# A weight block's first sum by an accumulating transfer, and seven products in four of eight row pairs of the MLPs

## The chip, the cores and the metric

The kernel runs on one core of one Trainium2 chip. The metric is device time in microseconds (us), as the median of repeated executions. The engines of the core are named as the profile names them: PE (TensorE, matrix multiplies; PEld its weight loads), DVE (VectorE), ACT (ScalarE), POOL (GpSimd) and SP (SyncE, which only issues transfers here). Transfers (DMA) are issued from a queue of SP or of POOL and share the core's 16 DMA engines.

## The reference

A decoder trunk of two layers over 256 positions of width 2048, all in float32. Layer 0 is retention with 8 heads, layer 1 latent attention with 16 heads; each is followed by an MLP with a squared ReLU of width 8192. Cut to what the change touches:

```python
def sq_relu_mlp(h, w1, w2):
    return jnp.square(jax.nn.relu(h @ w1)) @ w2

def reference(x, ...):
    for layer in range(2):
        if layer == 0:
            x = x + retention(rms_norm(x, norm_mix[0]), ret_w_in, ret_w_out, cos, sin)
        else:
            x = x + mla_attention(...)
        x = x + sq_relu_mlp(rms_norm(x, norm_mlp[layer]), mlp_w1[layer], mlp_w2[layer])
```

## The kernel before

**Float32 by two parts.** Each operand is split into a high part rounded for the PE (`wh`, a cast on ACT, line 185) and a low part (`wl`, the rest, a subtraction on DVE, line 186). A product of two 128-row blocks is then three matmuls: high by high, high by low, low by high (lines 356 to 358).

**Row pairs and column pairs.** The large weights stand in HBM as chunks of 1 MB, one for each row pair: 256 rows by 1024 columns, as four 128x512 blocks side by side in the order b11, b12, b22, b21 (128 partitions x 2048 elements). `gemm_pair` computes one column pair: it runs over its row pairs (eight in the MLPs), calls `quad` for each, and accumulates in PSUM. The 256 positions are two halves, so each row pair is a two-by-two block product. It takes eight products, or seven by a scheme of sums and differences of blocks: the activations' sums come from `with_sums` (line 392 on, kept in `more`), and the weights' sums are made in `quad`.

**One row pair in `quad`.** SP loads the chunk into `raw` (line 285; four buffers). For eight products there are two splits of 128x1024 and 24 matmuls. For seven there are four splits (128x1024, 128x512, 128x1024, 128x1024), three additions on DVE that make the weights' sums in place in `raw` (lines 321, 324, 325), and 21 matmuls. The parts have five buffers each (`wh`, `wl`), which bounds how far ACT and DVE run ahead of PE. `raw` is freed by its last split, and SP then loads the row pair that stands four further on.

**Which row pairs have seven.** `kinds` says it for each column pair. `THREE` is (3, 5, 7), `FOUR` is (1, 3, 5, 7), `HEAD` is (2, 4, 6, 7). Retention's gate and value projections (`rp`, one column pair a head) and the first half of its output projection (`ro`) use `HEAD`.

**The MLP.** `mlp` (line 784 on) walks four groups. A group has two column pairs of the up projection (`u`, p = 0 to 7 over the layer) and two of the down projection (`d`, p = 0 and 1), each over the group's eight row pairs. What ends an up pair (`pair_out`, `summed`, `up`, `turn`) runs in the first row pairs of the next column pair: ACT copies six accumulators out of PSUM (line 373), DVE joins them (lines 375 to 380 and 389), ACT applies the ReLU (797), PE transposes (205), ACT squares (806), and the blocks `hid` are split and, where a later seven needs it, summed (lines 396 to 398, `hid_sum`, `hid_more`).

**x's home.** The residual stream stands in HBM. A down pair that isn't of the last group adds its eight blocks there (`to_home`, line 150) by eight accumulating transfers of 256 KB from POOL's queue, also in the first row pairs of the next column pair; two go to each home block, and the second waits until the first has landed. The last group brings x back (`x_tiles`, line 140), adds, and writes it (line 474).

**Order.** Each engine works through its instructions in one fixed order, which a list scheduler chose when the program was built; an engine that waits holds up all that stands behind it. POOL's order holds the transfers that it issues and the small steps of the norms (lines 163 and 165).

Names: c11, c12, c21, c22 are the accumulators of the four result blocks, p1, p5, p6 and p7 those of the further products of the seven scheme, and u and v what `pair_out` joins from them.

Of the kernel before, what the change touches and what calls it, by code (L numbers as in the profile page):

```python
# [16 lines left out]
ALU = mybir.AluOpType  # L17
# [3 lines left out]
P = 128  # L21
# [25 lines left out]
NOPE, ROPE, MV, KVR, QR = 128, 64, 128, 512, 1536  # L47
KV_NBS, Q_NB = (320, 256), 384
GROUPS = (4, 4, 4, 4)
THREE, FOUR, HEAD = (3, 5, 7), (1, 3, 5, 7), (2, 4, 6, 7)  # L50
PI = math.pi

G_MIX0, G_MLP0, G_KV, G_MIX1, G_MLP1 = 0, 16, 32, 48, 64
# [15 lines left out]
def yoco(ctx: ExitStack, tc: tile.TileContext, a):  # L69
    nc = tc.nc  # L70
# [3 lines left out]
    def f2k(shape, name, dtype=F32):  # L74
        return pool.tile([P, *shape], dtype, tag="f2k", bufs=14, name=name)
# [15 lines left out]
    def act_tile(name, dtype=F32R):  # L91

        return pool.tile([P, 2, 2, S], dtype, tag="act", bufs=24, name=name)
# [5 lines left out]
    def later(n, fn):  # L99
        queue.append((clock[0] + n, next(count), fn))  # L100
# [11 lines left out]
    def need(items, n):  # L112
        while len(items) < n:
            run_first()
# [18 lines left out]
    def x_tiles(name):  # L133


        def bring(b):
            both = act_tile(f"x_{name}{b}", F32)
            for t in range(NT):
                x[t][b] = both[:, t].rearrange("p i s -> p (i s)")
                nc.gpsimd.dma_start(x[t][b], x_home[t][b])  # L140

        for b in range(NB):
            later(2 * b, lambda b=b: bring(b))
# [38 lines left out]
    def split(h, l, src, scale=None):  # L182

        if scale is None:
            nc.scalar.copy(h, src)  # L185
            nc.vector.tensor_tensor(l, src, h.bitcast(F32), op=ALU.subtract)  # L186
        else:
            nc.scalar.activation(h, src, AF.Copy, scale=scale)
            nc.vector.scalar_tensor_tensor(
                l, src, scale, h.bitcast(F32), op0=ALU.mult, op1=ALU.subtract  # L190
            )

    def split_act(v, src, scales=(None, None)):
        if scales == (None, None):
            split(v[:, :, 0], v[:, :, 1], src)
        else:
            for j in range(2):
                split(v[:, j, 0], v[:, j, 1], src[:, j], scales[j])

    def transposed(srcs, name):  # L200

        tp = bank("tp", [2, S], name)
        for j in range(2):
            for t in range(NT):
                nc.tensor.transpose(tp[:, j, t * P : (t + 1) * P], srcs(t, j), ident)
        return tp
# [75 lines left out]
    def quad(w, chunk, x, mm, name):  # L282

        raw = pool.tile([P, 2048], F32, tag="raw", bufs=4, name=f"{name}_raw")
        nc.sync.dma_start(raw, w[chunk])
        v, more = x

        def a(t, k):
            return [v[:, k, i, t * P : (t + 1) * P] for i in range(2)]

        def s(n):
            return [more[:, n // 2, i, n % 2 * P : (n % 2 + 1) * P] for i in range(2)]

        b = raw.rearrange("p (i n) -> p i n", i=4)

        def parts(src, part):
            n = src.free_size() // 512
            wh, wl = (
                pool.tile([P, 2, 512], F32R, tag=f"w{i}", bufs=5, name=f"{name}_w{i}{part}")[:, :n] for i in "hl"
            )  # L300
            split(wh, wl, src)
            return [[i[:, j] for i in (wh, wl)] for j in range(n)]

        b11, b22 = parts(b[:, 0:3:2], 0)
        if more is None:
            mm("c11", a(0, 0), b11)
            mm("c21", a(1, 0), b11)
            mm("c12", a(0, 1), b22)
            mm("c22", a(1, 1), b22)
            b12, b21 = parts(b[:, 1:4:2], 1)  # L310
            mm("c12", a(0, 0), b12)
            mm("c22", a(1, 0), b12)
            mm("c11", a(0, 1), b21)
            mm("c21", a(1, 1), b21)
            return
        mm("p1", a(0, 0), b11)
        mm("c12", s(3), b22)
        (b21,) = parts(b[:, 3:4], 1)
        mm("c11", a(0, 1), b21)

        nc.vector.tensor_tensor(  # L321
            b[:, 0:2], b[:, 0:3:2], b[:, 1].unsqueeze(1).to_broadcast([P, 2, 512]), op=ALU.add
        )
        nc.vector.tensor_tensor(b[:, 2], b[:, 0], b[:, 2], op=ALU.add)
        nc.vector.tensor_tensor(b[:, 3], b[:, 2], b[:, 3], op=ALU.add)
        u1, u3 = parts(b[:, 0:2], 2)
        mm("p5", s(1), u1)
        mm("p7", s(0), u3)
        u2, u4 = parts(b[:, 2:4], 3)
        mm("p6", s(2), u2)  # L330
        mm("c21", a(1, 1), u4)
# [53 lines left out]
    def summed(c):  # L385

        for row in c:
            for block in row:
                nc.vector.tensor_tensor(block[0], block[0], block[1], op=ALU.add)
        return [[block[0] for block in row] for row in c]  # L390

    def with_sums(blocks, name):

        blocks = blocks.rearrange("p j (t n) -> p (j t) n", t=NT)
        sums = f2k([4, P], f"{name}_sum")
        nc.vector.tensor_tensor(sums[:, 0:2], blocks[:, 0:2], blocks[:, 1:4:2], op=ALU.subtract)
        nc.vector.tensor_tensor(sums[:, 2], sums[:, 1], blocks[:, 0], op=ALU.subtract)
        nc.vector.tensor_tensor(sums[:, 3], blocks[:, 2], sums[:, 2], op=ALU.add)
        more = act_tile(f"{name}_more")
        split_act(more, sums.rearrange("p (j t) n -> p j (t n)", j=2))  # L400
        return more
# [4 lines left out]
    def gemm(w, chunk0, act, nk, nb, name, done, before=None):  # L406

        acc = accs(nb, name)
        n = nk // 4
        for g in range(n - 1):  # L410
            piece(w, chunk0 + g, acc, act, g, nk, nb, name, before)
        last_piece(w, chunk0, acc, act, nk, nb, name, done, before)
# [328 lines left out]
    for h in range(RH):  # L741
# [35 lines left out]
        kinds = HEAD if h > 1 else HEAD[1:]  # L777
# [6 lines left out]
    def mlp(layer, act, r, done):  # L784
        w1, w2 = a[f"mlp_w1_{layer}"], a[f"mlp_w2_{layer}"]
        f0 = 0
        for gi, nf in enumerate(GROUPS):
            hid, blocks = [], []
            last = gi == len(GROUPS) - 1

            def up(c, p, hid=hid, blocks=blocks, last=last):

                need(r, NT)
                c = summed(c)
                for t in range(NT):
                    for i in range(2):
                        nc.scalar.activation(c[t][i], c[t][i], AF.Relu, scale=r[t])

                def turn(i):
                    for q in (2 * i, 2 * i + 1):  # L800
                        name = f"hid{layer}_{p}{q}"
                        tp = transposed(
                            lambda t, j: c[t][q // 2][:, (q % 2 * 2 + j) * P : (q % 2 * 2 + j + 1) * P], f"{name}_tp"
                        )
                        u = f2k([2, S], f"{name}_u")
                        nc.scalar.activation(u, tp, AF.Square)
                        v = act_tile(name)
                        split_act(v, u)
                        blocks.append((v, with_sums(u, name) if len(blocks) in (THREE if last else FOUR) else None))
                        hid.append(v)  # L810

                later(0, lambda: turn(0))
                later(1, lambda: turn(1))

            for p in range(f0 // 2, (f0 + nf) // 2):
                kinds = THREE[not (p or layer) :] if p % 2 or not p else FOUR
                gemm_pair(
                    w1, p * 8, act, [i in kinds for i in range(8)], f"u{layer}_{p}", lambda c, p=p, up=up: up(c, p)
                )
            if last:  # L820
                x_tiles(f"mlp{layer}")
            for p in range(2):
                if last and p and layer:
                    for b in (2, 3):
                        need(hid, 2 * nf)
                        gemm(
                            a["mlp_w2t"], (b - 2) * nf, hid, 4 * nf, 512, f"d{layer}_{gi}{b}",
                            lambda acc, b=b: done(b, acc),
                        )
                    continue  # L830

                def add(c, p=p, last=last):
                    into_x(done, c, p) if last else to_home(c, p)

                kinds = [i in (FOUR if p and not last else THREE) for i in range(2 * nf)]
                gemm_pair(w2, p * 32 + 2 * f0, blocks, kinds, f"d{layer}_{gi}{p}", add)
            f0 += nf

# [347 lines left out]
```

## Time and profile before

| | us |
|---|---|
| median of 3 runs | 2477.24 (2477.16 to 2477.25) |
| profiled execution | 2474.51 |
| its span | 2472.7 |

The profile is of one execution. Its span runs from the first to the last instruction of the program. In its lists, "L321 DVE u_raw<-u_raw" is the work of line 321 of the kernel on DVE, with buffer numbers left out of the names; a row ends with a count, busy time and mean, or, in a timeline, with the idle time before it and what ended that. What the stages take in the span:

| stage | us from the span's start |
|---|---|
| inputs, first head's gate | 0 to 90 |
| retention, heads | 90 to 625 |
| its output projection, second half | 625 to 720 |
| MLP of layer 0 | 720 to 1396 |
| latent attention | 1396 to 1770 |
| MLP of layer 1 | 1770 to 2472 |

The lines of the page on transfers and its list of transfer issues:

```profile
DMA  9555567555564685684785564445545856857854
GB/s 328 211 174 205 196 205 234 199 192 201 198 236 182 209 262 216 213 254 172 246 263 196 192 228 168 153 155 179 199 174 199 261 212 209 268 203 225 266 192 153
...
u_raw<-in_mlp_w SPq DMA_DIRECT2D x128, 1024.0 KB, 5.2
d_raw<-in_mlp_w SPq DMA_DIRECT2D x120, 1024.0 KB, 4.9
rp_raw<-in_ret_w_gv SPq DMA_DIRECT2D x56, 1024.0 KB, 4.9
```

The first row has the mean busy share of the 16 DMA engines in tenths, in 40 slices of the span. In the last three rows stand the count, the size, and the median us from issue to landing.

### The profile page before, as it was taken

Reading aid. Unit: us, or ns where it says so; the run is one execution under the profiler, and the core shown is the slowest. Engines: PE = TensorE matmul, PEld = TensorE weight load, DVE = VectorE, ACT = ScalarE, POOL = GpSimd, SP = SyncE. Lnnn points to the kernel's source line nnn. Section 1 sums busy time; section 2 is a strip of 40 time slices with the busy share of each in tenths; the row PEclk is TensorE's granted clock in tenths of the full one; section 3 lists DMA queues with packets and bytes.
Section 4 is the critical chain, followed back from the end, with each engine's and each line's share of the span. In section 5 each row is a group of like instructions: output and inputs, shape, how many; then the busy total and the mean of one; then the engine's idle time right before and its main releaser. Section 6 shows DMA issues by size and latency. Waiting matters only on the chain.

```text
span 2472.7 us, 31711 instructions
## 1 busy us (share of the span) xinstructions
PE 2455.6 (99%) x11635; PEld 2060.0 (83%) x11635; DVE 2167.4 (88%) x2805; ACT 1606.1 (65%) x2253; POOL 251.6 (10%) x310
## 2 busy tenths in 40 slices
PE   9999999999999999999999999999999999999999
PEld 7888888888888888888888888998888888888887
DVE  7799899889899999999999967776689999999996
ACT  6566656556676667667666766676566666676663
POOL 7300011000010010110110101110000201101100
PEclk9999999999999999999999999999999999999999
DMA  9555567555564685684785564445545856857854
GB/s 328 211 174 205 196 205 234 199 192 201 198 236 182 209 262 216 213 254 172 246 263 196 192 228 168 153 155 179 199 174 199 261 212 209 268 203 225 266 192 153
DMA packets 93403, 521.04 MB, mean 211 GB/s; under 512 B 11072, under 2 KB 12224, under 8 KB 40000
## 3 DMA queue, kind: packets, MB, share of 16 engines
q1 hardware_dynamic: 71856, 472.83, 53.8%
q0 software_dynamic: 21248, 46.15, 8.5%
q8 instruction: 91, 1.49, 0.2%
q14 instruction: 64, 0.52, 0.1%
q10 hardware_dynamic: 144, 0.05, 0.0%
HBM read 479.14 MB, written 39.85 MB: 210 GB/s over the span
## 4 chain that ended last, share of the span: by engine, by line
PE 91%; DVE 4%; ACT 3%; issue 1%; POOL 1%; DMA 0%; SPq 0%; ACTq 0%; POOLq 0%; DVEq 0%
PE u_c L358 7%; PE u_c L356 7%; PE u_c L357 7%; PE d_c L357 6%; PE d_c L358 6%; PE d_c L356 6%; PE rk_acc L274 2%; PE rq_acc L274 2%; PE rp_c L356 2%; PE rp_c L357 2%; PE rp_c L358 2%; PE u_p L358 2%; PE u_p L356 2%; PE u_p L357 2%; PE d_p L356 2%; PE d_p L358 2%
## 5 line engine op out<-in xcount | busy, mean ns | idle before, releaser
L185 ACT CAST u_wh<-u_raw 128x1024 fp32r<-128x1024 f32 x362 | 347.9, 991 | 207.8 <-DVE u_raw L321 100.8
L185 ACT CAST d_wh<-d_raw 128x1024 fp32r<-128x1024 f32 x358 | 344.1, 993 | 202.5 <-DVE d_raw L321 93.9
L186 DVE TENSOR_TENSOR u_wl<-u_raw,u_wh 128x1024 fp32r<-128x1024 f32 x362 | 402.0, 1144 | 47.2 <-ACT u_wh L185 41.7
L186 DVE TENSOR_TENSOR d_wl<-d_raw,d_wh 128x1024 fp32r<-128x1024 f32 x358 | 397.8, 1146 | 40.1 <-ACT d_wh L185 35.5
L356 PE MATMUL u_c<-u_wh,n 128*128 128x512 f32 x706 | 276.4, 392 | 0.0
L357 PE MATMUL u_c<-u_wl,n 128*128 128x512 f32 x706 | 275.5, 390 | 0.0
L358 PE MATMUL u_c<-u_wh,n 128*128 128x512 f32 x706 | 274.9, 389 | 0.0
L356 PE MATMUL d_c<-d_wh,hid 128*128 128x512 f32 x654 | 256.0, 392 | 0.0
L357 PE MATMUL d_c<-d_wl,hid 128*128 128x512 f32 x654 | 255.4, 391 | 0.0
L358 PE MATMUL d_c<-d_wh,hid 128*128 128x512 f32 x654 | 254.6, 389 | 0.0
L185 ACT CAST rp_wh<-rp_raw 128x1024 fp32r<-128x1024 f32 (+1 forms) x166 | 160.7, 982 | 140.9 <-DVE rp_raw L321 64.9
L186 DVE TENSOR_TENSOR rp_wl<-rp_raw,rp_wh 128x1024 fp32r<-128x1024 f32 (+1 forms) x166 | 184.9, 1137 | 26.7 <-ACT rp_wh L185 24.4
L358 PEld LDWEIGHTS u_c<-u_wh,n 128*128 128x128 f32 x706 | 132.6, 188 | 27.4
L356 PEld LDWEIGHTS u_c<-u_wh,n 128*128 128x128 f32 x706 | 132.6, 188 | 26.9
L357 PEld LDWEIGHTS u_c<-u_wl,n 128*128 128x128 f32 x706 | 132.6, 188 | 26.7
L358 PEld LDWEIGHTS d_c<-d_wh,hid 128*128 128x128 f32 x654 | 122.8, 188 | 25.4
L356 PEld LDWEIGHTS d_c<-d_wh,hid 128*128 128x128 f32 x654 | 122.8, 188 | 25.2
L357 PEld LDWEIGHTS d_c<-d_wl,hid 128*128 128x128 f32 x654 | 122.9, 188 | 24.7
L150 POOL DMA_DIRECT2D xh<-d_c x48 | 41.6, 867 | 856.6 <-ACT d_c L373 854.7
L185 ACT CAST ro_wh<-ro_raw 128x1024 fp32r<-128x1024 f32 x88 | 85.7, 997 | 59.7 <-DVE ro_raw L321 25.7
L356 PE MATMUL rp_c<-rp_wh,a 128*128 128x512 f32 x286 | 111.9, 391 | 0.0
L357 PE MATMUL rp_c<-rp_wl,a 128*128 128x512 f32 x286 | 111.4, 390 | 0.2 <-DVE rp_wl L186 0.2
(465 smaller groups left out, 6075.6 us busy)
## 6 DMA issues: line engine op xcount, KB each, us to landing
u_raw<-in_mlp_w SPq DMA_DIRECT2D x128, 1024.0 KB, 5.2
d_raw<-in_mlp_w SPq DMA_DIRECT2D x120, 1024.0 KB, 4.9
rp_raw<-in_ret_w_gv SPq DMA_DIRECT2D x56, 1024.0 KB, 4.9
ro_raw<-in_ret_w_out SPq DMA_DIRECT2D x32, 1024.0 KB, 4.9
uq_raw<-in_mla_w_uq SPq DMA_DIRECT2D x24, 768.0 KB, 4.1
rq_raw<-in_ret_w_qk SPq DMA_DIRECT2D x16, 1024.0 KB, 5.0
rk_raw<-in_ret_w_qk SPq DMA_DIRECT2D x16, 1024.0 KB, 4.8
wo_raw<-in_mla_w_o SPq DMA_DIRECT2D x16, 1024.0 KB, 4.8
```

Source lines behind the costliest of these rows:

```text
L150: nc.gpsimd.dma_start(x_home[t][2 * p + j], part, accum_op=ALU.add)
L185: nc.scalar.copy(h, src)
L186: nc.vector.tensor_tensor(l, src, h.bitcast(F32), op=ALU.subtract)
L274: nc.tensor.matmul(acc[f], wh[:, cols], a.rearrange("p i s -> p (i s)"), start=k == 0, stop=k == nk - 1)
L356: nc.tensor.matmul(dst, ah, bh, start=n == 0, stop=False)
L357: nc.tensor.matmul(dst, ah, bl, start=False, stop=False)
L358: nc.tensor.matmul(dst, al, bh, start=False, stop=n == total[key] - 1)
```

## The change

1. In `quad`, where a row pair has seven products, POOL issues an accumulating transfer inside SBUF that adds b11 to b12 in place (256 KB), in every stage that uses sevens. The first DVE addition, which made b11 + b12 and b12 + b22 at 128x1024, goes. DVE now adds b22 to that sum (128x512), takes b11 off again for b12 + b22 (128x512), and adds b21 as before (128x512). The two sums change places in `raw`, so `u1` and `u3` are named the other way round.
2. `FOUR` becomes (2, 3, 5, 7). It also says which activation blocks have sums, so block 2 has them in place of block 1.
3. In the MLPs, all up pairs but p = 0 use `FOUR` (before, the odd ones and p = 0 used `THREE`; in layer 0, p = 0 has (5, 7) before and after), and all down pairs but the last group's use `FOUR` (before, only p = 1). That is 14 more row pairs with seven: 157 in place of 143 in the whole kernel.

```diff
-THREE, FOUR, HEAD = (3, 5, 7), (1, 3, 5, 7), (2, 4, 6, 7)
+THREE, FOUR, HEAD = (3, 5, 7), (2, 3, 5, 7), (2, 4, 6, 7)
...
         nc.sync.dma_start(raw, w[chunk])
         v, more = x
+        if more is not None:
+            nc.gpsimd.dma_start(raw[:, 512:1024], raw[:, 0:512], accum_op=ALU.add)
...
-        nc.vector.tensor_tensor(
-            b[:, 0:2], b[:, 0:3:2], b[:, 1].unsqueeze(1).to_broadcast([P, 2, 512]), op=ALU.add
-        )
-        nc.vector.tensor_tensor(b[:, 2], b[:, 0], b[:, 2], op=ALU.add)
+        nc.vector.tensor_tensor(b[:, 2], b[:, 1], b[:, 2], op=ALU.add)
+        nc.vector.tensor_tensor(b[:, 0], b[:, 2], b[:, 0], op=ALU.subtract)
         nc.vector.tensor_tensor(b[:, 3], b[:, 2], b[:, 3], op=ALU.add)
-        u1, u3 = parts(b[:, 0:2], 2)
+        u3, u1 = parts(b[:, 0:2], 2)
...
-                kinds = THREE[not (p or layer) :] if p % 2 or not p else FOUR
+                kinds = FOUR if p else THREE[1 - layer :]
...
-                kinds = [i in (FOUR if p and not last else THREE) for i in range(2 * nf)]
+                kinds = [i in (THREE if last else FOUR) for i in range(2 * nf)]
```

In the changed kernel the transfer is line 288 and the three additions are lines 323, 324 and 325. In the built program's order on POOL, in a column pair that follows a down pair, the transfer for row pair 2 stands behind the first home transfer, the one for row pair 3 behind the third, and those for row pairs 5 and 7 behind all eight.

## The prediction

> **What bounds the kernel now.** I read the page first, then stage windows, then TensorE's timeline matmul by matmul.
>
> ```profile
> span 2472.7 us, 31711 instructions
> ...
> PE 2455.6 (99%) x11635; PEld 2060.0 (83%) x11635; DVE 2167.4 (88%) x2805; ACT 1606.1 (65%) x2253; POOL 251.6 (10%) x310
> ...
> PE 91%; DVE 4%; ACT 3%; issue 1%; POOL 1%; DMA 0%; SPq 0%; ACTq 0%; POOLq 0%; DVEq 0%
> ```
>
> TensorE is busy nearly throughout and owns 91% of the chain that ended last. Since a busy PE is not PE at its peak, I checked its beat in a row pair of seven products:
>
> ```profile
> 1041.35 0.39 PE L357 MATMUL d_c<-d_wl,hid 128*128 128x512 f32 x1
> ...
> 1045.88 0.39 PE L356 MATMUL d_c<-d_wh,hid 128*128 128x512 f32 x1
> ```
>
> Twenty matmuls lie between these two starts, 4.53 us, so one every 0.2265 us: back to back. What takes a matmul away pays; what makes PE wait costs its full length. DVE is the next limit, and it differs by kind of column pair:
>
> ```profile
> 929.00:972.00 43.00, 43.00 (x199) 35.42 (x198) 40.85 (x52) 31.35 (x42) 0.00 (x0) 1.00 0.53 187
> 972.00:1016.00 44.00, 44.00 (x203) 36.27 (x202) 41.85 (x52) 31.35 (x42) 0.00 (x0) 1.00 0.54 196
> 1016.00:1057.00 41.00, 41.00 (x183) 33.91 (x182) 38.34 (x42) 25.43 (x30) 6.96 (x8) 1.00 0.87 264
> ```
>
> The columns are us, then PE, PEld, DVE, ACT, POOL busy, clock, DMA share, GB/s. The first two windows are pairs that follow an up pair (u0_3, d0_10): DVE is busy 95%, because the relu'd blocks are turned, split and summed there. The third (d0_11) follows a down pair: DVE has 2.7 us left, but the transfers to x's home (L150) run and the 16 DMA engines are 87% busy. The granted clock is 1.00 in all three.
>
> **The change, part by part.** *Products.* Of the MLPs' column pairs, 14 go from three to four row pairs with seven products (u odd: 4, d p=0 of three groups: 3, in each of two layers). Each saves one product of three matmuls: 14 x 3 x 0.2265 = **9.5 us less PE**. The casts that go with it on ACT are hidden: ACT has 11 us and more idle in each window. FOUR's 1 becoming 2 moves a block's sums and adds none: nothing, since the same number of blocks is summed in the same stretch.
>
> *The sum by transfer.* All 157 row pairs of seven get an accumulating transfer of 256 KB (L288) on POOL's queue, and DVE's 128x1024 add becomes 128x512. That takes about 0.5 us of DVE from each. Where DVE holds PE up this pays. The idle time of weight loads at L270, the start of a head, shows it:
>
> ```profile
>   DVE rq_wl L186: 4.0, 11
> ```
>
> Head kinds (2,4,6,7) end in two sevens, and DVE is late there by up to 0.4 us a head; four cheaper sevens remove it. Between 0 and 4.0 us I take **3 us**. Retention's rstd steps (L163, L165) on POOL now have L288s between them; POOL is busy 10% and each of these waits only for its own block's load, issued some row pairs ahead, so I count nothing, and under 1 us a head if a load is late, with DVE's y behind it.
>
> *DVE in pairs after an up pair.* This is where the 14 mostly lie: u odd (8) and d p=0 (6). In u0_3 as it is:
>
> ```profile
> 947.12 2.35 DVE L186 TENSOR_TENSOR u_wl<-u_raw,u_wh 128x1024 fp32r<-128x1024 f32 x2
> ...
> 951.93 1.22 DVE L321 TENSOR_TENSOR u_raw<-u_raw 128x1024 f32<-128x1024 f32 x1
> 953.07 0.69 DVE L186 TENSOR_TENSOR hid_more<-hid_sum,hid_more 128x512 fp32r<-128x512 f32 x1
> ...
> 956.99 2.35 DVE L186 TENSOR_TENSOR u_wl<-u_raw,u_wh 128x1024 fp32r<-128x1024 f32 x2
> ```
> ```profile
> 959.74 0.39 PE L357 MATMUL u_p<-u_wl,n_more 128*128 128x512 f32 x1
> ```
>
> Row pair 3's third low part is ready at 956.99 + 1.22 = 958.21 and first used at 959.74: 1.53 us to spare, with DVE working without a gap since the pair's start (ACT's copies out of PSUM tie that start to PE, so DVE can't run ahead of it). Now row pair 2 becomes a seven as well, in front of this point. A 128x1024 step takes 1.14 us of DVE (951.93 to 953.07); as an eight it has two, 2.28. As a seven it has three such splits, one 128x512 split at 0.61 and three 128x512 adds at 0.72, 0.72, 0.61 (spacings of L324 and L325 in the rows below): 6.1, so 3.8 more. Row pair 3's cheaper add gives back 0.5. PE arrives 0.68 earlier. 1.53 - 3.3 - 0.68 = -2.45; in the new order the second `hid_more` split stands ahead of this point too (0.6), -3.05. I take 2.6 us of PE wait in 12 pairs and 1.3 in u0_7 and u1_7, where one sum less is made: **34 us**. Nothing gives it back: PE is back to back after it.
>
> *Does the transfer come in time?* Row pair 7 of u0_3, the tightest without home transfers:
>
> ```profile
> 959.37 0.33 SPq L285 DMA_DIRECT2D u_raw<-in_mlp_w  x1
> DMA to landing us min/median/max: 4.8/4.8/4.8
> ...
> 973.25 1.22 DVE L321 TENSOR_TENSOR u_raw<-u_raw 128x1024 f32<-128x1024 f32 x1
> ```
>
> It lands at 964.2 and DVE adds at 973.25: 9.0 us. No transfer in SBUF is in the trace; the nearest is L150's accumulate of the same size. Into an empty queue it took 7.4 and 6.7 us from issue to landing (below). So it hides there. The order on POOL is the trouble in the 12 pairs with home transfers:
>
> ```profile
> 1021.40 0.86 POOL L150 DMA_DIRECT2D xh<-d_c  x1 [111.14 <-ACT d_c L373]
> 1023.85 0.86 POOL L150 DMA_DIRECT2D xh<-d_c  x1 [1.59 <-ACT d_c L373]
> 1025.28 0.86 POOL L150 DMA_DIRECT2D xh<-d_c  x1 [0.57 <-ACT d_c L373]
> 1027.25 0.86 POOL L150 DMA_DIRECT2D xh<-d_c  x1 [1.10 <-ACT d_c L373]
> 1035.29 0.86 POOL L150 DMA_DIRECT2D xh<-d_p  x1 [7.18 <-DMA xh<-d_c]
> 1036.27 0.86 POOL L150 DMA_DIRECT2D xh<-d_u  x1
> 1036.81 1.22 POOL L150 DMA_DIRECT2D xh<-d_v  x1
> 1037.35 1.57 POOL L150 DMA_DIRECT2D xh<-d_p  x1
> ...
> DMA to landing us min/median/max: 7.4/7.4/7.4
> ...
> DMA to landing us min/median/max: 6.7/9.8/11.8
> ...
> 1026.39 0.39 PE L357 MATMUL d_c<-d_wl,hid 128*128 128x512 f32 x1
> ...
> 1054.27 0.39 PE L357 MATMUL d_p<-d_wl,hid_more 128*128 128x512 f32 x1
> ```
>
> The landing rows are of the first transfer and of the last four. Those four, issued within 2.1 us, land from 1042.0 to 1049.2: one each 2.4 us, in order. Call the pair's first use of a low part, 1026.39, zero. The new order on POOL between two down pairs is: c22, *row pair 2*, c12, c11, *row pair 3*, p1, c21, v, u, p5, *row pair 5*, *row pair 7* (italics are L288). p1 waits for c11 to land, as at 1035.29 now, and u for c21, which is now issued behind p1. With 2.4 us each: c22 lands at 2.4, row pair 2 at 4.8, c12 7.2, c11 9.6, row pair 3 at 12.0; p1 is issued at 10.0 and lands at 16.7, c21 19.1, v 21.5; u is issued at 19.5 and lands at 26.2, p5 28.6, **row pair 5 at 31.0**. From the second down pair to the next up pair c21 stays ahead of p1, and the same walk gives 28.7. When is it wanted?
>
> ```profile
> 1047.75 1.22 DVE L321 TENSOR_TENSOR d_raw<-d_raw 128x1024 f32<-128x1024 f32 x1
> 1049.01 0.69 DVE L324 TENSOR_TENSOR d_raw<-d_raw 128x512 f32<-128x512 f32 x1
> 1049.73 0.69 DVE L325 TENSOR_TENSOR d_raw<-d_raw 128x512 f32<-128x512 f32 x1
> 1050.34 2.50 DVE L186 TENSOR_TENSOR d_wl<-d_raw,d_wh 128x1024 fp32r<-128x1024 f32 x2
> ```
>
> DVE reaches this add at 21.4 today, and PE uses the result at 1054.27, 27.9; PE's place is the same after the change (two sevens ahead of it either way). The new chain to the split's end is two adds of 0.72, ACT's cast of about 1.0, a split of 1.22, some 3.8. So the transfer must land by 24.1; behind L323 every later split waits, and PE behind those. The walk gives 6.9 and 4.6 us of PE wait. Bounds: with 1.5 us each (below) 1.5 and nothing, with 2.9 each 9.9 and 8.6. While DVE stands, weight loads stop for want of buffers and leave the engines to this queue, so I take a little under the walk, 5 us: 12 x 5 = **60 us** (9 to 111).
>
> ```profile
> q0 software_dynamic: 21248, 46.15, 8.5%
> ```
>
> 8.5% of 2472.7 us over 176 transfers is 1.2 us of all 16 engines each, so an accumulate has hardly less; four more a pair add 0.12 or more to the 0.87 above: close to full, which is why I don't take the lower bound.
>
> [...]
>
> *Retention's output projection.* Its two column pairs before rp4 have the same batch, with row pair 4's transfer right behind v:
>
> ```profile
> 362.30 1.21 POOL L150 DMA_DIRECT2D xh<-ro_v  x1
> ...
> DMA to landing us min/median/max: 10.4/11.1/11.8
> ...
> 373.43 0.39 PE L357 MATMUL ro_p<-ro_wl,y_more 128*128 128x512 f32 x1
> ```
>
> v lands at 372.7; two transfers of 2.4 more (row pair 2's ahead, and its own) give 377.5, against 373.43 - 3.8 = 369.6: 8 us. I take 7 for each of two: **14 us** (0 to 18).
>
> *Sum:* 2474.5 (the profiled execution, span 2472.7 within it) - 9.5 - 3 + 34 + 60 + 14 = 2570. The runs' median lies 2.7 us above that execution: **2573 us**.
>
> **The rivals.** *(A) Transfers hidden, DVE late.* If an accumulate in SBUF needs under about 1.2 us in the queue, only the 34 us stay: 2474.5 - 12.5 + 34 + 2.7 = 2499. For it: no HBM in the path. Against: engine time is no smaller. [...] *(B) Faster: all waits hidden, PE bound.* 2474.5 - 12.5 + 2.7 = 2465. It needs row pair 5 landed by 24.1 and over 2.6 us of DVE that I count as busy to be free; DVE's total does fall (143 x 0.5 less, 14 x 4 more), but not where it is short. *(C) Engines full.* At 2.9 us each the batches cost 111 and 18, with 34: 2474.5 - 12.5 + 163 + 2.7 = 2628; the point is a DMA share at 1.0 in those pairs.
>
> **How the numbers follow.** Forecast 0.62, A 0.16, C 0.12, B 0.10. Within B and between B and A lies about 0.03 for no change, of 0.2% or 5 us, about what this measurement can tell: faster 0.09, same 0.03, slower 0.88. The forecast's own range is 2530 to 2610. The 8 in 10 range takes in A and most of C: 2490 to 2622, leaving out B and C's end.
>
> **What would show it.** Right: 42 matmuls fewer at the same 0.2265 us beat; DVE's L323 idle, ended by DMA, some 5 us in each of 12 pairs, always row pair 5 behind p5's L150; PE idle ended by DVE's low part of row pair 3 in pairs after an up pair, 2 to 3 us. Wrong: landings of L288 under 5 us behind L150, DMA idle at L323 only in single us, or PE still at 99% of its span with no DVE waits. The heads' L270 waits should fall from 4.0 us to about 1.

## The result, and the profile after

| | us |
|---|---|
| before, median of 6 runs beside it | 2477.2 (2475.1 to 2479.5) |
| after, median of 6 runs | 2631.0 (2624.9 to 2635.7) |
| ratio | 1.062 (95% interval 1.061 to 1.064) |
| profiled execution after | 2631.3, span 2629.4 |

The change costs 154 us. The forecast was 2573 with a range to 2622: the right side, and short by more than a third of the move.

The page of the changed kernel: span, TensorE, its granted clock over 40 slices, POOL's queue, and the chain of waits by engine.

```profile
span 2629.4 us, 32282 instructions
...
PE 2510.3 (95%) x11593; PEld 2079.4 (79%) x11593; DVE 2138.7 (81%) x2875; ACT 1613.6 (61%) x2281; POOL 383.9 (15%) x467
...
PEclk9999999999999989999999999999999899899999
...
PE 59%; DVE 15%; DMA 13%; ACT 5%; issue 4%; POOL 2%; ACTq 0%; POOLq 0%; SPq 0%; DVEq 0%
```

There are 42 matmuls fewer (11635 before), yet PE is busy 55 us longer: some matmuls take longer, and the row PEclk says where to look. The granted clock is no longer full in every slice, as it was in the kernel before:

```profile
PEclk9999999999999999999999999999999999999999
```

PE's share of the chain fell from 91% to 59%, and DMA, which was absent, has 13%.

What PE waits for, in the list of waits (us in total, times, longest):

```profile
PE d_p L356 <- ACT d_wh L185: 51.3, 12, 7.3
PE u_p L356 <- ACT u_wh L185: 23.0, 13, 3.0
```

The long ones are the first matmul of p5 (L356, `u1` by `s(1)`), the first use of a part that is made from the sums. The waits are put down to ACT's cast, but ACT itself waited for DVE's L324. Followed back in the column pair d0_01 (d with p=1, after a down pair), on POOL and on DVE:

```profile
898.45 0.85 POOL L150 DMA_DIRECT2D xh<-d_p  x1 [7.71 <-DMA xh<-d_c]
...
907.25 0.85 POOL L150 DMA_DIRECT2D xh<-d_u  x1 [6.18 <-DMA xh<-d_c]
907.79 1.19 POOL L150 DMA_DIRECT2D xh<-d_p  x1
908.33 1.54 POOL L288 DMA_DIRECT2D d_raw<-d_raw  x1
```
```profile
919.28 0.69 DVE L323 TENSOR_TENSOR d_raw<-d_raw 128x512 f32<-128x512 f32 x1 [9.66 <-DMA d_raw<-d_raw]
```

Row pair 5's transfer is issued directly behind p5's, after POOL has waited twice for a first home transfer, and DVE's L323 stands 9.66 us for it. What PE does with that:

```profile
914.38 0.39 PE L358 MATMUL d_c<-d_wh,hid 128*128 128x512 f32 x1
921.96 0.80 PE L356 MATMUL d_p<-d_wh,hid_more 128*128 128x512 f32 x1 [7.19 <-ACT d_wh L185]
923.22 0.80 PE L357 MATMUL d_p<-d_wl,hid_more 128*128 128x512 f32 x1 [0.47 <-DVE d_wl L186]
...
927.23 0.63 PE L357 MATMUL d_c<-d_wl,hid 128*128 128x512 f32 x1
927.65 0.46 PE L358 MATMUL d_c<-d_wh,hid 128*128 128x512 f32 x1
927.95 0.39 PE L356 MATMUL d_c<-d_wh,hid 128*128 128x512 f32 x1
```

After 7 us of standing, matmuls start 0.42 to 0.43 us apart up to 927.65, and then come back to 0.2265. The same place in windows (us, PE, PEld, DVE, ACT, POOL busy, clock, DMA share, GB/s):

```profile
914.00:916.00 2.00, 0.77 (x4) 0.31 (x2) 0.00 (x0) 0.00 (x0) 0.18 (x1) 1.00 1.08 313
916.00:918.00 2.00, 0.00 (x0) 0.00 (x0) 0.00 (x0) 0.00 (x0) 0.00 (x0) 0.88 1.11 201
918.00:920.00 2.00, 0.00 (x0) 0.00 (x0) 0.69 (x1) 0.00 (x0) 0.00 (x0) 0.50 0.61 110
...
926.00:928.00 2.00, 2.00 (x7) 1.57 (x6) 2.00 (x3) 0.38 (x1) 0.00 (x0) 0.56 0.96 393
928.00:930.00 2.00, 2.00 (x10) 1.64 (x9) 1.97 (x4) 0.20 (x1) 0.00 (x0) 1.00 1.08 410
```

The granted clock falls to 0.50 some 3 us into the wait (the trace's record of the clock has 917.53) and comes back at 927.77, 5.8 us after PE has work again. PE counts as busy in that time, which is where most of its 55 us came from.

To size this everywhere I took the start of every matmul from the timeline of the whole span and subtracted the usual distance to the next (the median for that line and accumulator). Excess over 0.3 us is summed as wait, smaller excess as slow beat:

| wait / slow beat, us | before | after | e1 transfer alone | e2 kinds alone | e3 row 5 by DVE | e4 home later | e7 unwaited |
|---|---|---|---|---|---|---|---|
| 14 pairs after an up pair | 0 / 0.5 | 33.7 / 18.6 | 0 / 0.6 | 41.6 / 25.7 | 35.6 / 18.3 | 36.9 / 19.3 | 0 / 0.6 |
| 12 pairs after a down pair | 0 / -0.6 | 69.4 / 21.2 | 50.7 / 15.8 | 0 / 0.1 | 9.9 / 4.0 | 26.2 / 5.1 | 0 / -0.4 |
| second output projection pair, head 4 | 0.7 / 0.3 | 13.7 / 3.7 | 15.2 / 3.2 | 0.7 / 0.4 | 8.9 / 2.4 | 7.0 / 2.4 | 0.7 / 0.3 |
| head 1 | 0.9 / 0.3 | 5.7 / 0.9 | 6.0 / 1.0 | 0.9 / 0.3 | 5.5 / 0.9 | 5.4 / 0.9 | 1.6 / 0.4 |
| the heads' start (rq) | 1.6 / 0.7 | 0 / -0.4 | 0 / -0.4 | 1.7 / 0.7 | 0 / 0 | 0 / 0 | 1.6 / 0.2 |

Over the whole kernel the excess is 164.5 us more after than before. Less 42 x 0.2265 = 9.5 that is 155; the spans differ by 156.7.

### The profile page after: what moved, and what is told of

Its sections match the earlier page's. It is cut to its first block, busy times and chain, and to the rows that moved or that the text cites. A ratio compares the mean times of both kernels' runs of the same rounds, so it can differ in the third digit from the quotient of the medians.

```text
span 2629.4 us, 32282 instructions
## 1 busy us (share of the span) xinstructions
PE 2510.3 (95%) x11593; PEld 2079.4 (79%) x11593; DVE 2138.7 (81%) x2875; ACT 1613.6 (61%) x2281; POOL 383.9 (15%) x467
## 3 DMA queue, kind: packets, MB, share of 16 engines
q0 software_dynamic: 43856, 87.32, 17.4%
## 4 chain that ended last, share of the span: by engine, by line
PE 59%; DVE 15%; DMA 13%; ACT 5%; issue 4%; POOL 2%; ACTq 0%; POOLq 0%; SPq 0%; DVEq 0%
DMA xh<-d_c 5%; PE u_c L356 3%; PE u_c L357 3%; PE u_c L358 3%; PE d_c L356 3%; PE d_c L357 3%; PE d_c L358 3%; DVE u_wl L186 2%; DMA d_raw<-d_raw 2%; DVE d_wl L186 2%; DMA u_raw<-u_raw 2%; PE rq_acc L274 2%; PE rp_c L358 2%; PE rp_c L356 2%; PE rp_c L357 2%
## 5 line engine op out<-in xcount | busy, mean ns | idle before, releaser
L186 DVE TENSOR_TENSOR u_wl<-u_raw,u_wh 128x1024 fp32r<-128x1024 f32 x378 | 413.8, 1135 | 79.6 <-ACT u_wh L185 78.5
L356 PE MATMUL u_c<-u_wh,n 128*128 128x512 f32 x658 | 260.8, 396 | 3.3 <-ACT u_wh L185 3.3
L357 PE MATMUL u_c<-u_wl,n 128*128 128x512 f32 x658 | 258.3, 393 | 0.0
L358 PE MATMUL u_c<-u_wh,n 128*128 128x512 f32 x658 | 257.8, 392 | 0.0
L356 PE MATMUL d_c<-d_wh,hid 128*128 128x512 f32 x618 | 245.0, 396 | 2.9 <-ACT d_wh L185 2.9
L357 PE MATMUL d_c<-d_wl,hid 128*128 128x512 f32 x618 | 242.7, 393 | 0.0
L358 PE MATMUL d_c<-d_wh,hid 128*128 128x512 f32 x618 | 241.7, 391 | 0.0
L356 PEld LDWEIGHTS u_c<-u_wh,n 128*128 128x128 f32 x658 | 125.2, 190 | 32.3 <-ACT u_wh L185 6.8
L358 PEld LDWEIGHTS u_c<-u_wh,n 128*128 128x128 f32 x658 | 124.8, 190 | 26.6
L357 PEld LDWEIGHTS u_c<-u_wl,n 128*128 128x128 f32 x658 | 125.2, 190 | 25.7
L356 PEld LDWEIGHTS d_c<-d_wh,hid 128*128 128x128 f32 x618 | 117.6, 190 | 29.7 <-ACT d_wh L185 5.5
L358 PEld LDWEIGHTS d_c<-d_wh,hid 128*128 128x128 f32 x618 | 117.2, 190 | 24.8
L288 POOL DMA_DIRECT2D u_raw<-u_raw x61 | 58.9, 966 | 467.5 <-DVE u_raw L324 161.6
L356 PE MATMUL d_p<-d_wh,hid_more 128*128 128x512 f32 x171 | 72.9, 432 | 51.3 <-ACT d_wh L185 51.3
L288 POOL DMA_DIRECT2D d_raw<-d_raw x57 | 54.4, 954 | 403.6 <-DVE d_raw L324 113.6
```

Source lines behind the costliest of these rows:

```text
L288: nc.gpsimd.dma_start(raw[:, 512:1024], raw[:, 0:512], accum_op=ALU.add)
L356: nc.tensor.matmul(dst, ah, bh, start=n == 0, stop=False)
L357: nc.tensor.matmul(dst, ah, bl, start=False, stop=False)
L358: nc.tensor.matmul(dst, al, bh, start=False, stop=n == total[key] - 1)
```

## The experiments

Times are medians beside runs of the kernel before on the same chip (2475.6 to 2476.4).

**e1, the transfer alone.** The 14 column pairs go back to three sevens.

```diff
-                kinds = FOUR if p else THREE[1 - layer :]
+                kinds = THREE[not (p or layer) :] if p % 2 or not p else FOUR
...
-                kinds = [i in (THREE if last else FOUR) for i in range(2 * nf)]
+                kinds = [i in (FOUR if p and not last else THREE) for i in range(2 * nf)]
```

> The sum by transfer stays everywhere; the 14 column pairs go back to three sevens (u odd, d p=0). Theory: those 14 pairs then have no PE wait (in the changed kernel they hold 33 us of idle before row pair 3's p5, and 18 us of matmuls at a slow beat behind it), 42 matmuls come back (9.5 us), and the waits before row pair 5 after a down pair and before row pair 4 in retention stay: 2631 - 51 + 9.5, 2580 to 2597 us. Rival, the transfers stretch the engines' own work wherever they run: the 14 pairs keep 2 us of wait or more each, over 2610 us.

2557.9 us (2550.6 to 2565.1), ratio 1.033 (1.026 to 1.040). The 14 pairs have no wait at all (table), though three transfers run beside each: that part holds. It is faster than I expected, since the wait before row pair 5 also shrank, from 69 to 51 us. But POOL's order is not the changed kernel's in this build: in the six d pairs (p=1), row pair 2's transfer stands ahead of the first home transfer and c21 ahead of p1, and there the wait fell from 50.7 to 17.9 us. In the six u pairs the order is the changed kernel's, and there it rose from 18.7 to 32.8; why is not shown. So this run prices the transfer without the kinds, but under another order in half of the pairs.

**e2, the kinds alone.** No transfer, the three additions of before.

```diff
-        if more is not None:
-            nc.gpsimd.dma_start(raw[:, 512:1024], raw[:, 0:512], accum_op=ALU.add)
...
-        nc.vector.tensor_tensor(b[:, 2], b[:, 1], b[:, 2], op=ALU.add)
-        nc.vector.tensor_tensor(b[:, 0], b[:, 2], b[:, 0], op=ALU.subtract)
+        nc.vector.tensor_tensor(
+            b[:, 0:2], b[:, 0:3:2], b[:, 1].unsqueeze(1).to_broadcast([P, 2, 512]), op=ALU.add
+        )
+        nc.vector.tensor_tensor(b[:, 2], b[:, 0], b[:, 2], op=ALU.add)
```

> No transfer: the sums are made by the three DVE additions of before, the kinds are those of the changed kernel. Theory: the 12 pairs after a down pair and retention have no wait beyond before's; the 14 pairs after an up pair wait longer than with the transfer, since each of the two sevens ahead of row pair 3's use costs DVE 0.5 us more: 3.4 to 4.4 us idle each and up to 1.9 us of slow beat behind it. 2477 - 9.5 + 48 to 62 + 18 to 27: 2530 to 2557 us. Rival, the waits in these pairs come from the transfers too and not from DVE's work: under 2490 us.

2534.0 us (2532.4 to 2535.5), ratio 1.023 (1.020 to 1.026): the theory's side, with waits of 3.0 us a pair where I expected 3.4 to 4.4. PE's waits of this kernel:

```profile
PE u_p L356 <- ACT u_wh L185: 15.1, 10, 2.1
PE d_p L356 <- ACT d_wh L185: 9.0, 7, 1.4
```

They are DVE's shortage and need no transfer; with the transfer the same pairs wait 8 us less in all (33.7 against 41.6). The two halves cost 82 and 58 us alone and 154 together.

**e3, row pair 5 by DVE.** Where the home transfers stand ahead, the sum is made by DVE as before.

```diff
+LATE = [f"d{i}_{g}1" for i in range(2) for g in range(3)] + [f"u{i}_{p}" for i in range(2) for p in (2, 4, 6)]
+BY_DVE = {f"{i}5" for i in LATE} | {"ro014", "rp44"}
...
+        by_dve = name in BY_DVE
-        if more is not None:
+        if more is not None and not by_dve:
...
```

> The changed kernel, but row pair 5 in the 12 pairs after a down pair and row pair 4 in the second output projection pair and in the pair of head 4 are summed by DVE as before, with no transfer. Theory, these transfers are late because they stand behind the home transfers on POOL: their waits (69 + 14 us idle) and the slow beat behind them (21 + 4) go, the rest stays: 2631 - 107, 2518 to 2535 us. Rival, the 16 DMA engines have no room for the sums at all: the next transfer of the pair is late in its place, over 2570 us.

2547.1 us (2546.7 to 2547.6), ratio 1.029 (1.026 to 1.032): between the two. In the 12 pairs 90.6 us of wait and slow beat became 13.9, but the output projection and head 4 kept 11.3 of 17.4: row pair 6's transfer is late in row pair 4's place. DVE's waits in this kernel:

```profile
DVE rp_raw L334 <- DMA rp_raw<-rp_raw: 12.0, 2, 6.7
...
DVE ro_raw L334 <- DMA ro_raw<-ro_raw: 7.5, 1, 7.5
```

L334 is the addition that follows a transfer. In `ro` it is now row pair 6's: issued when its load has landed, at 376.6, the transfer needs 13.2 us to land, behind the last home transfers, which POOL issued from 369.9 to 371.0. The rival's pattern, then, in two pairs of fourteen.

**e4, the home transfers later.** All sums by transfer and the same bytes; only p1, u, v and p5 go behind row pair 5's transfer on POOL (in the d pairs, c21 thereby stands ahead of p1).

```diff
...
+        def half(i):
+            for j in range(2):
+                for t in range(NT):
+                    nc.gpsimd.dma_start(x_home[t][2 * p + j], c[t][j][i], accum_op=ALU.add)
+        def second():
+            with tc.issue_after(last_sum[0].ins):
+                half(1)
+        half(0)
+        later(5, second)
...
```

> The changed kernel, all sums by transfer, but the second four home transfers of a down pair (p1, u, v, p5) are put on POOL behind the transfer of row pair 5 (row pair 4 in retention). The bytes moved are the same. Theory, order on POOL: row pair 5's sum lands within 8 us of its load's landing, its wait goes, and row pair 7's, which now stands behind the four, lands in time or 1 to 2 us late: 2518 to 2550 us. Rival, no room in the DMA engines: row pair 5 or 7 waits as long as row pair 5 did, over 2590 us.

2559.6 us (2553.0 to 2566.1), ratio 1.034 (1.027 to 1.040). POOL in d0_01 (L296 is the sum's transfer, L151 home's):

```profile
890.39 0.85 POOL L296 DMA_DIRECT2D d_raw<-d_raw  x1 [8.42 <-DMA d_raw<-in_mlp_w]
890.94 1.19 POOL L151 DMA_DIRECT2D xh<-d_p  x1
...
904.49 0.86 POOL L296 DMA_DIRECT2D d_raw<-d_raw  x1 [9.60 <-DMA d_raw<-in_mlp_w]
```

And DVE's L331, the addition that needs the transfer, in row pairs 5 and 7:

```profile
899.96 0.68 DVE L331 TENSOR_TENSOR d_raw<-d_raw 128x512 f32<-128x512 f32 x1
...
913.45 0.69 DVE L331 TENSOR_TENSOR d_raw<-d_raw 128x512 f32<-128x512 f32 x1 [4.47 <-DMA d_raw<-d_raw]
```

Row pair 5's transfer, now ahead of the four, lands 5.1 us after its issue and 4.5 us before DVE wants it. The order on POOL alone takes 59 of the 12 pairs' 90.6 us. What stays, 31 us, sits in other row pairs: here row pair 7's transfer, issued when its load has landed at 904.5, needs 8.9 us, and PE waits 1.9. These 31 us, and 9.4 in retention's two pairs, where I expected none, put the time above the expected 2518 to 2550.

**e5, transfers meant for nobody.** Before, with each of its 143 sevens sending b11 to a spare block of HBM (`nc.gpsimd.dma_start(spare, raw[:, 0:512], accum_op=ALU.add)`), DVE's additions as they were.

> The kernel before, with 143 more accumulating transfers of 256 KB from POOL's queue, at the places of the changed kernel's, from b11 into a block of HBM that nothing reads; DVE's sums as before. Only the next load of the same buffer waits for them. Theory: a transfer costs only where its landing is waited for, so the time stays within 0.3% of before, under 2485 us. Rival, the transfers take DMA time from the weight loads or slow the engines by themselves: 3 us in each of the 14 pairs beside home transfers or 0.3 us for each transfer, 2515 us and more.

2584.0 us (2577.7 to 2590.1), ratio 1.043 (1.040 to 1.045): far above what I expected, and by a fault of the experiment. DVE's in-place sums overwrite b11, so they must wait until the transfer has read it:

```profile
DVE d_raw L324 <- DMA spare<-d_raw: 47.5, 6, 9.4
```

The wait was not gone but changed its reason. It still shows that a transfer in this place costs a like amount when its reading is waited for and not its sum (62.0 and 23.5 us of wait and slow beat in the 12 pairs, 69.4 and 21.2 in the changed kernel).

**e7, transfers that nothing waits for.** The same transfer for the 193 row pairs of eight instead, whose blocks no engine overwrites.

```diff
+        if more is None:
+            nc.gpsimd.dma_start(spare, raw[:, 0:512], accum_op=ALU.add)
...
```

> The kernel before, with an accumulating transfer of 256 KB from b11 into a block of HBM that nothing reads for each of the 193 row pairs of eight products, whose blocks no engine overwrites: only the next load of the same buffer waits for such a transfer. Theory, a transfer costs what is waited for at its landing and little by itself: under 2490 us. Rival, 193 transfers take DMA time from the loads or slow the engines by 0.3 us each or more: over 2530 us.

2478.0 us (10 runs, 2476.9 to 2482.1), ratio 1.001 (1.000 to 1.002). Its page, and the windows of two pairs after a down pair (d0_01, u0_2):

```profile
q0 software_dynamic: 49120, 97.02, 22.0%
```
```profile
860.00:901.00 41.00, 41.00 (x183) 33.91 (x182) 38.33 (x41) 25.62 (x32) 7.52 (x9) 1.00 0.99 281
901.00:942.00 41.00, 41.00 (x182) 33.92 (x181) 38.30 (x42) 25.63 (x30) 10.89 (x13) 1.00 1.02 284
```

More bytes on POOL's queue than the changed kernel has (97 against 87 MB), engines that are busy 99 to 102% in these windows, and PE works through both without a gap. So full DMA engines alone cost PE nothing here. How far they stretch a landing that is waited for, this run does not say; the landings themselves are compared with the rival's below.

**e6 and e8, PE kept busy while it waits.** Matmuls of zeros into p5's accumulator stand directly ahead of the matmul that waits; e6 has 130 of them in 22 pairs, e8 only the three in each of twelve pairs after an up pair.

```diff
+        for _ in range(WARM.get(name, 0)):
+            mm.fill(cst[:, C_MASK + P : C_MASK + 2 * P], cst[:, 0:256])
         mm("p5", s(1), u1)
...
+        def fill(zero, some):
+            nc.tensor.matmul(get("p5")[:, 0:256], zero, some, start=False, stop=False)
```

> The changed kernel with 130 more matmuls (128x256 f32, zeros by anything, added to p5's accumulator) that stand in PE's order right before the waiting matmul: 13 in each of six d pairs with p=1 (some 5.8 us of the 7 us wait), 4 in u2 and u4 of both layers, 3 in twelve of the pairs after an up pair. Theory: the waits end when they ended, but PE's granted clock stays at 1.00, so the matmuls behind the wait keep their 0.2265 us beat, and the time falls by the 30 us that the slow beat costs in these 22 pairs: 2592 to 2610 us. Rival, the slow beat behind a wait has another cause (weights that arrive one by one, transfers beside it): the time stays at 2631 or rises.

> The changed kernel with 36 more matmuls (128x256 f32, zeros by anything, added to p5's accumulator), three in each of twelve column pairs after an up pair, ahead of the matmul that waits for row pair 3's parts; POOL's order is the changed kernel's. Theory: the wait's end stays, and where the granted clock fell behind it in the changed kernel (9 of the 12 pairs) the pair is 1.6 us shorter: 2631 - 14, 2611 to 2622 us. Rival, the slow beat is not tied to PE standing idle: 2627 us or more.

e6: 2627.3 us (2618.8 to 2636.4), no change as a whole, where I expected 2592 to 2610. In its build POOL's order differs too (in the pairs from down to up, row pair 2's transfer now stands ahead of the first home transfer), and u0_6 and u1_6, which have no added matmul, became 8.6 and 9.0 us longer. So e8 leaves those pairs alone: 2625.3 us (2624.2 to 2628.7), against 2631.0 for the changed kernel, ratio to before 1.060 (1.059 to 1.062). That is less than expected in sum (2611 to 2622), but clear pair by pair. u0_1 of the changed kernel, then of e8:

```profile
811.57 0.39 PE L358 MATMUL u_c<-u_wh,n 128*128 128x512 f32 x1
813.73 0.73 PE L356 MATMUL u_p<-u_wh,n_more 128*128 128x512 f32 x2 [1.77 <-ACT u_wh L185]
...
817.11 0.63 PE L356 MATMUL u_p<-u_wh,n_more 128*128 128x512 f32 x1
817.53 0.63 PE L357 MATMUL u_p<-u_wl,n_more 128*128 128x512 f32 x1
```
```profile
811.92 0.40 PE L363 MATMUL u_c<-u_wh,n 128*128 128x512 f32 x1
812.16 1.46 PE L366 MATMUL u_p<-cst 128*128 128x256 f32 x6
814.08 0.73 PE L361 MATMUL u_p<-u_wh,n_more 128*128 128x512 f32 x2 [0.46 <-ACT u_wh L188]
...
816.56 0.39 PE L361 MATMUL u_p<-u_wh,n_more 128*128 128x512 f32 x1
816.79 0.39 PE L362 MATMUL u_p<-u_wl,n_more 128*128 128x512 f32 x1
```

The wait ends at the same distance (2.16 us from the start of the row pair's last earlier matmul in both: 811.57 to 813.73, 811.92 to 814.08), but behind it the beat is 0.43 us in the one and 0.23 in the other. The eight pairs that had the slow beat in the changed kernel (u0_1, d0_00, d0_10, d0_20, u1_1, d1_00, d1_10, u1_5; I had expected nine) are 1.5 to 1.6 us shorter each, 12.8 in all, in e6 by the same; of the four that had none, three stay within 0.02 us and one is 0.3 longer. What e8 loses again is in the pairs after a down pair, whose landings moved (+6.8 us in sum). Added work made these pairs faster; the slow beat is the clock's. The traces' records of the granted clock agree: of these twelve pairs it falls in exactly those eight in the changed kernel, and in none in e8.

**b1 to b4, is there a version that gains?** b1: before, up pairs at (3, 5, 6, 7), the sum by transfer in odd up pairs and in heads 2, 3, 5, 6, 7; b2: the same with DVE's sums in the up pairs; b3: before with the transfer in those heads alone; b4: before with the transfer in every column pair that has no home transfers beside it but head 1 and d0_31. All of them choose by name:

```diff
+        by_dma = name[:-1] in BY_DMA
+        if more is not None and by_dma:
+            nc.gpsimd.dma_start(raw[:, 512:1024], raw[:, 0:512], accum_op=ALU.add)
...
```

> The kernel before with all up pairs but p=0 at (3, 5, 6, 7), the activations' sums for these blocks, the sum by transfer only in the odd up pairs and in heads 2, 3, 5, 6 and 7 (no home transfers beside any of them), and DVE's additions elsewhere; down pairs as before. Theory: after an up pair DVE is short only ahead of row pair 3's use; later sevens find it ahead again, so 8 products less (5.4 us) and the heads' 2.3 us show: 2467 to 2473 us. Rival, three sevens in a row leave DVE late at row pair 7 by 1 to 2 us in 8 pairs, with a slow beat behind: 2485 to 2505 us.

> As the run beside it, but the odd up pairs are summed by DVE too (transfers in heads 2, 3, 5, 6 and 7 alone). Each of their sevens costs DVE 0.5 us more. Theory: DVE falls behind by up to 1.85 us in each of the three last sevens and has about 4.5 us in hand before them, so it is late by some 1 us in 8 pairs: 2475 to 2490 us. Rival, DVE has more in hand: 2467 to 2473 us, and the transfer isn't needed there.

> The kernel before, with the sum by transfer in heads 2, 3, 5, 6 and 7 alone (20 transfers, no home transfers beside them). Theory: these land in time, DVE has 0.5 us less in each of four sevens, and the head's start no longer waits for its low part: 2.3 us less, 2474 us, a ratio of 0.9990. Rival, the heads' waits are not DVE's: 2476 to 2478 us.

> The kernel before, with the sum by transfer in every column pair that has no home transfers beside it (heads 2, 3, 5, 6, 7, three output projection pairs, u with p=0 and odd, d with p=0; kinds as before). Theory: all of these land in time and only the heads' waits go, as in the run beside it: 2474 us. Rival, some pair has less room for a landing than the heads: each late landing adds its length and up to 2 us of slow beat, 2480 us or more.

b1 2500.9 us (ratio 1.010, 1.008 to 1.011) is on its rival's side; b2 2501.6 (1.010, 1.009 to 1.012) is slower than its theory (2475 to 2490) and its rival had it. Every up pair but p = 0 now waits 1.1 to 2.7 us, in its last row pairs, the even ones too. So DVE looks short over the whole pair with sevens at these places, and not only ahead of row pair 3; on DVE itself that was not measured. b3 2474.7 and b4 2473.9, both 0.9996 (0.9988 or 0.9987 to 1.0005) of before: the transfer is hidden in all of these pairs and gains nothing that can be told from no change. No version that beats the kernel before was found.

## Why the prediction was wrong, step by step

- *Products:* right, 42 matmuls and 9.5 us.
- *The heads' starts:* right in size (3 taken, 2.7 measured; the idle time at L270 fell from 4.0 to 0.7), though b3 shows that such an amount does not stand out in the time.
- *DVE in pairs after an up pair, 34 us:* the wait is 33.7. PE is released by ACT's cast behind DVE's L324 and not by the low part itself, which follows 0.5 us later.
- *Row pair 5, 60 us:* the wait is 69.4. The walk along POOL's queue gave 6.9 and 4.6 us a pair, 69 in all; I lowered it to 5 because a standing DVE would free the engines. That discount was wrong in sum. The split was not exact either: about 8.4 us in d pairs (50.7 over six), 3.1 in u pairs. Counted as in the walk, row pair 5's transfer landed at 31.7 to 32.4 in the d pairs (walk 31.0) and at 24.8 to 28.1 in the u pairs (walk 28.7). That the walk's sum came out to 0.4 us is luck in part: the landings are not 2.4 us apart but 1.2 to 4.8, as in the d pairs, where p5 lands some 2 us later than walked and the sum only 1.2 to 1.3 us behind it.
- *Retention's output projection, 14 us:* 13.0 more than before.
- *rstd on POOL, "nothing, and under 1 us a head":* wrong in head 1, by 5.4 us. There it is not the rstd steps but the tables that POOL makes in that time; row pair 4's transfer stands behind the last of them:

```profile
114.48 0.29 POOL L521 TENSOR_SCALAR tm_rr<-tm_rr 128x128 f32<-128x128 f32 x1
115.08 1.84 POOL L288 DMA_DIRECT2D rp_raw<-rp_raw  x2 [0.31 <-issue]
```
```profile
123.64 0.69 DVE L323 TENSOR_TENSOR rp_raw<-rp_raw 128x512 f32<-128x512 f32 x1 [6.93 <-DMA rp_raw<-rp_raw]
```

- **The step that failed** is in the first part: "what makes PE wait costs its full length", and with it "PE is back to back after it". A wait here costs its length and then, in most cases, some 2 us more at half clock, a term that the prediction does not have. From the table, against before: 18.1 us in the 14 pairs, 21.8 in the 12, 3.4 in retention, 43 in all.

The sum closes: forecast 2570 against the profiled 2631, 61 us short. Of these 43 are the slow beat, 9.4 the discount on the walk, 5.4 head 1; the rest, about 3, is spread. No row of the kernel before could show the first: it has no wait over 2 us on PE in these pairs, and its clock row is full throughout.

Rival C came within 3 us of the measured time by its number, 2628, and is wrong. At its 2.9 us a transfer, an estimate of mine, row pair 5's sum would have landed at 34.0 in the d pairs and 32.7 in the u pairs, later than any did, and PE would have waited 111 us in the 12 pairs, where it waited 69. In e4 the same bytes in another order took 59 of these pairs' 90.6 us away, and in e7 full engines alone cost nothing. Its number came near because waits that are 47 us too long (163 against 116 in the same places) stand in for the 43 us of slow beat, which it lacks too. A near number is no evidence for a cause. Rival A, 2499, had the transfers hidden: in the changed kernel L288's landing takes 3.2 us from issue at best and 6.3 in the median, and DVE's L323 waits 106.7 us for these landings in all, 81.2 of them in the MLPs.

## What to carry to other kernels

A stall of TensorE is to be priced at its length plus what was measured behind it, here some 2 us at half clock (43 us; the changed kernel's record of the clock has 21 falls, 20 of them in the pairs of the table); in eight of these kernels all 43 stalls of 2 us and more came with half clock, in e6 one of 2.16 us did not, and shorter ones did in part. A transfer was free here as long as nothing waited for its landing (193 that nobody needs cost 0.1%, and in b4 the sums that land in time nothing that shows), and dear where it stood behind others in one queue (90.6 us in the 12 pairs, of which e4's order took 59): walk the queue's order, with one landing per transfer, before the bytes. And where an engine is short in one stretch, moving work to later row pairs of the same pair helps only if its total there fits.

## What the runs showed of the hardware

- **In these traces the changes of the granted clock lay whole multiples of 3.41 us apart, and whether it fell went with how long PE had stood in the step before.** The wait of u0_1, shown above, and this one of u0_3 in the changed kernel are equal to 0.01 us, and behind this one the beat stays at 0.23:

```profile
1004.87 0.39 PE L358 MATMUL u_c<-u_wh,n 128*128 128x512 f32 x1
1007.02 0.73 PE L356 MATMUL u_p<-u_wh,n_more 128*128 128x512 f32 x2 [1.77 <-ACT u_wh L185]
```

In eight kernels (after, e1 to e5, b1, b2), half clock came with all 43 waits of PE of 2.0 us and more (a matmul every 0.4267 us in place of 0.2265), with the shorter ones only in part; in e6 one of 2.16 us came without it. The traces' records of the granted clock show what sorts them. In the ten kernels in which it falls before the end (these, e6 and e8), its changes lie whole multiples of 3.41 us apart, to 0.004 us. Where PE stood (the time outside its busy rows) under 1.4 us in such a step, none of 7183 steps at full clock was followed by half clock; from 1.4 to 2.0 us, 30 of 62 were; from 2.0 us on, all 72. In the changed kernel alone these are none of 703, 7 of 11 and all 14. The two waits in these steps (columns as above):

```profile
811.72:815.13 3.41, 1.15 (x5) 0.48 (x4) 3.38 (x6) 2.49 (x4) 0.00 (x0) 1.00 0.00 0
815.13:818.55 3.42, 3.42 (x9) 2.64 (x10) 3.42 (x4) 3.13 (x4) 0.00 (x0) 0.50 0.37 98
```
```profile
1002.86:1006.28 3.42, 2.39 (x11) 1.66 (x9) 3.39 (x7) 1.61 (x4) 0.00 (x0) 1.00 0.22 91
1006.28:1009.69 3.41, 2.18 (x8) 1.53 (x9) 3.41 (x5) 3.24 (x4) 0.00 (x0) 1.00 0.00 0
1009.69:1013.10 3.41, 3.41 (x16) 2.82 (x16) 3.41 (x4) 1.87 (x3) 0.00 (x0) 1.00 0.74 243
```

In u0_1 one step has 2.26 us without PE, and the clock falls at its end, 1.4 us after the wait is over (813.73). In u0_3 the same wait is cut in two, 1.03 and 1.23 us, and nothing falls. The half clock lasted whole steps: 3.41 us in u0_1 and 10.24 in d0_01, where PE stands in the first 4.4.
- **Nearly equal builds need not have equal queues.** 130 added matmuls changed the order on POOL, and two column pairs without any of them became 9 us longer; in e1, other kinds in 14 pairs changed it in six others. A comparison by the total alone would have hidden that the twelve pairs in question did what was expected.
